# Modulation vectors summed on VectorE instead of TensorE, their weights in a ring of four tiles, and every high part of a weight made by ScalarE

## The chip, the cores and the metric

One NeuronCore of a Trainium2 chip runs the whole program. The metric is the device time of one execution in microseconds. Five engines work side by side, each with its own queue, in order: TensorE (PE; its weight loads are shown as PEld), VectorE (DVE), ScalarE (ACT), GpSimd (POOL) and SyncE (SP), which here issues the DMA transfers. TensorE reads SBUF and writes PSUM; a PSUM tile of this kernel holds 1024 fp32 columns, and there are four of them.

## The reference

A two-layer trunk is run on 640 tokens: 128 context tokens and 512 latent tokens. Each group has its own conditioning vector, and each layer makes six modulation vectors of 1024 numbers from it, for both groups:

```python
def adaln(cond, w, b):
    m = jax.nn.silu(cond) @ w + b                      # w: 1024 x 6144, per layer
    return [m[:, None, i * D_MODEL:(i + 1) * D_MODEL] for i in range(N_MOD)]

def trunk_layer(x, mods, l, P, angs, ctx_k, ctx_v):
    sh1, sc1, g1, sh2, sc2, g2 = mods
    hn = rmsnorm(x, P['norm1_g'][l]) * (1 + sc1) + sh1
    mix, k, v = token_mixer(hn, l, P, angs, ctx_k, ctx_v)   # attention, Fourier mixer, gates, w_o
    x = x + g1 * mix
    hn = rmsnorm(x, P['norm2_g'][l]) * (1 + sc2) + sh2
    return x + g2 * channel_mixer(hn, l, P), k, v           # w_up, 3-tap convolution, silu gate, w_down
```

All data are fp32. The modulation vectors depend on the two conditioning vectors alone, not on the tokens, so their product with w (24 MB per layer) can be made at any time before its use.

## The kernel before

Activations lie transposed, channels on partitions and the 640 tokens along the free axis, in two chunks of 320. A product of fp32 precision is made of three fp32r products: weight and activation are each split into a high part (the value rounded to fp32r) and a low part (the rest), and `proj` (line 358) issues for each block of 128 input channels and each chunk high x high, high x low and low x high into PSUM: six matmuls of 320 columns per block of input channels. After each such block it calls `tick` (line 348), the clock of all side work.

Weights come in blocks of mostly 1 MB in the order of `make_plan` (line 71) through two raw tiles (`pump_loads`, line 286). `queue_split` (line 298) lists, for each 512 columns of the next block, one function that makes the high part `w_h` (line 311 on ScalarE, line 313 on GpSimd) and one that makes the low part `w_l` by subtraction on VectorE (line 317). A tick issues one of them, and one function of the queue `q` of epilogues. During the attention ScalarE makes all high parts; elsewhere ScalarE and GpSimd take turns.

```python
self.hcount += 1
if self.heads_on or self.hcount % 2:
    nc.scalar.copy(out=h[:, a:b], in_=raw[:, a:b])
else:
    nc.gpsimd.tensor_scalar(out=h[:, a:b], in0=raw[:, a:b], scalar1=1.0, scalar2=0.0, ...)
```

The modulation vectors are cut in blocks of 512 columns, 12 per layer. The first four of layer 0 are made in the prologue. The other 20 are made here by `ada_half` (line 399): a half holds 512 of the 1024 input channels, which come as one 1 MB block through the same raw tiles as the weights. Four matmuls with the conditioning vectors as weights (128x32, of which two columns are used) lie side by side in four column strips of the array and stream 512 columns each, in fp32; the profile shows two instructions for each. The first half's sums are copied to SBUF (line 407), the second's added (line 411); then four transposes, a reduction over the strips (line 429) and the addition of the bias (line 416) give four columns of `c_mods` for both groups. 12 halves lie in each layer's attention, four in each layer's gates, and the eight of the four blocks that layer 1's first norm needs lie in layer 0's feed-forward part, one after each up-projection job from the second on.

A layer runs so (`layer`, line 1244): attention, eight heads of five units each, whose steps (scores, softmax on VectorE and ScalarE, transposes, product with the values) alternate with the projections for the next head as filler by a written cost; then the gates stage, eight jobs of two projections each, with the Fourier mixer's steps between them; `merge` (Fourier and attention projections and the gates' products); `w_o` with the update of x; the feed-forward part, eleven pairs of up-projection jobs (22 tiles of 128 channels for values, 22 for gates) with the convolution (line 945 on ScalarE, line 940 twice on VectorE), and down-projections in three rounds after the fifth, eighth and eleventh pair. At the three norm boundaries `hold` keeps new splits back while the norm's steps run.

In the gates the projections alternate between the two PSUM tiles `ps_d`, and a sigmoid (line 786) frees each; the Fourier mixer uses the other two. In the merge and feed-forward parts projections go round all four tiles (`psq`).

The other intermediate tiles are 53 numbered slots of 640 columns, handed out first in, first out by `alloc` and `give`. The tables (rotary cosine and sine, Fourier matrices) have a tile of their own, `c_big`, loaded once by one DMA. The code's order is a priority and not yet the queues': a list scheduler under the tile framework orders each engine's queue, so that an instruction whose inputs are there can stand ahead of one that the code issues earlier.

Of the kernel before, what the change touches and what calls it, by code (L numbers as in the profile page):

```python
# [12 lines left out]
AF = mybir.ActivationFunctionType  # L13
# [14 lines left out]
NSLOT = 53  # L28
# [3 lines left out]
FILL = (1.3, .5, 1.1, 1.1)  # L32
FF_ROUNDS = ((0, 8), (8, 6), (14, 8))
# [37 lines left out]
def make_plan():  # L71
# [10 lines left out]
    def ada(l, cb):  # L82
        return [(("ada", l, cb, r), "ada", "w_ada", l, 512 * r, 4, [(512 * cb, 512)]) for r in range(2)]

# [6 lines left out]
    def ada_next():  # L91
        if adaq:
            add(*adaq.popleft())

    adaq = deque()
    for l in range(DEPTH):
        kq(l, 0)
        v(l, 0)
        for cb in range(4, 12):
            adaq.extend(ada(l, cb))  # L100
        for h in range(8):
            if h < 7:
                kq(l, h + 1)
                ada_next()
                if h < 6 and h % 2 == 0:
                    v(l, h // 2 + 1)
                    ada_next()
            else:
                for i in range(2):
                    w(("f", l, i), "w_in", l, 0, 8, [(256 * i, 256)])  # L110
                    ada_next()
        for i in range(4):
            for g in range(2):
                w(("g", l, g, i), "w_in", l, 0, 8, [(3584 + 1024 * g + 256 * i, 256)])
                ada_next()
        assert not adaq
# [6 lines left out]
        if l == 0:  # L123
            for cb in (2, 3, 0, 1):
                adaq.extend(ada(1, cb))

        def up(j):
            for g in range(2):
                w(("up", l, g, j), "w_up", l, 0, 8, [(DFF * g + 256 * j, 256)])
                if j:  # L130
                    ada_next()
# [16 lines left out]


# [11 lines left out]
def lay_out(inputs):  # L161
# [4 lines left out]
    for l in range(DEPTH):  # L166
# [7 lines left out]
        "w_first": np.stack([np.stack([block(g, src, 4) for src in b]) for b in FIRST_ADA]),  # L174
        "w_stream": np.concatenate([block(g, src, shape[0]).reshape(-1) for _, src, shape, _ in make_plan()]),
# [8 lines left out]
class Kern:  # L184
    def __init__(self, tc, st, I, O):
# [9 lines left out]
        self.big = mk("c_big", [128, 2560])  # L195
        self.ident = self.small
        b = self.big
        self.cos, self.sin = b[:, 0:512], b[:, 512:1024]
        self.csj = b[:, 1024:1280]
        self.c128, self.s128 = b[:, 1280:1408], b[:, 1408:1536]  # L200
        self.ttab = [b[:, 1536 + 256 * i:1792 + 256 * i] for i in range(4)]
        self.one = mk("c_one", [128, 1])
# [16 lines left out]
        self.q = deque()  # L219
        self.plan = make_plan()  # L220
# [5 lines left out]
        self.wseq = [i for i in range(self.n) if self.plan[i][3] == "w"]  # L226
# [6 lines left out]
        self.hcount = 0  # L233
        self.heads_on = False
        self.out_job = None
        self.psi = 0

# [60 lines left out]
    def queue_split(self, j):  # L298
# [1108 lines left out]
```

## Time and profile before

| | |
|---|---|
| median of 3 runs | 2242.63 us (2241.78 to 2243.69) |
| profiled execution, its own time | 2242.44 us |
| its span, first to last instruction | 2240.7 us |
| mean granted TensorE clock | 0.994 of 2.4 GHz |
| busy: PE / PEld | 2185.7 us (98%) / 2102.7 us (94%) |
| busy: DVE / ACT / POOL | 1225.3 (55%) / 800.2 (36%) / 362.4 us (16%) |
| DMA | 200.41 MB, mean 89 GB/s |

The stages of the span, in us: prologue to 72, attention of layer 0 to 380, gates to 500, merge and w_o to 672, feed-forward to 1126, boundary to 1170, attention of layer 1 to 1480, gates to 1600, merge and w_o to 1772, feed-forward to the end. Busy times of engines overlap; that of PE counts from a matmul's start to its modelled end, and matmuls are pipelined, so neighbours overlap too. An engine's idle time costs nothing as long as another engine sets the end.

### The profile page before, as it was taken

The page shows a single profiled execution, that of the slowest core. Times are in us where ns is not written, and L with a number is a line of the kernel's source. Part 1 is how long each engine was busy: PE and PEld are TensorE (multiplying, and loading weights), DVE is VectorE, ACT ScalarE, POOL GpSimd, SP SyncE. Part 2 cuts the span into 40 slices and gives each one's busy share as a digit, 9 for nine tenths or more (in the row PEclk, how much of TensorE's full clock was granted, in tenths as well). Part 3 has the DMA queues.
Part 4 walks back from the last instruction along what each step waited for, and adds up shares of the span by engine and source line. Part 5 has one row for each costly group of instructions (what it writes and reads, how often), then busy time and mean ns, then how long its engine had stood idle before and what let it go on. Part 6 is the DMA issues. An engine that isn't in the chain of part 4 may idle for free.

```text
span 2240.7 us, 36749 instructions
## 1 busy us (share of the span) xinstructions
PE 2185.7 (98%) x15142; PEld 2102.7 (94%) x15142; DVE 1225.3 (55%) x2258; ACT 800.2 (36%) x1601; POOL 362.4 (16%) x560
## 2 busy tenths in 40 slices
PE   7999999999999999999999999999999999999998
PEld 5988989999999999999989888899999999999997
DVE  5776675225456544545476766742344765355454
ACT  4565564212134221313246666532211433122221
POOL 2122122001032000000051211210010410000001
PEclk9999999999999999999999999999999999999999
DMA  8222322222213332122212222222222122222221
GB/s 312 84 84 84 118 79 76 113 94 71 73 66 113 133 112 76 62 90 76 76 66 102 83 82 85 79 112 99 91 76 76 59 76 75 75 77 75 76 76 47
DMA packets 40631, 200.41 MB, mean 89 GB/s; under 512 B 4496, under 2 KB 12048, under 8 KB 19344
## 3 DMA queue, kind: packets, MB, share of 16 engines
q1 hardware_dynamic: 40464, 198.07, 25.1%
q8 instruction: 119, 1.95, 0.4%
q14 instruction: 48, 0.39, 0.1%
HBM read 193.33 MB, written 4.72 MB: 88 GB/s over the span
## 4 chain that ended last, share of the span: by engine, by line
PE 76%; issue 7%; DVE 5%; POOL 5%; ACT 5%; DMA 1%; SPq 0%; POOLq 0%; ACTq 0%; DVEq 0%
PE ps_d L267 43%; PE ps_t L267 16%; PE ps_s L267 16%; POOL slot L500 2%; POOL ors L703 1%; ACT slot L634 1%; PE ps_t L270 1%; DVE nm L632 1%; DMA slot<-in_w_first 1%; ACT slot L536 1%; ACT junk L701 1%; DVE slot L515 1%; POOL oms L702 1%; ACT slot L537 1%; DVE w_l L317 1%
## 5 line engine op out<-in xcount | busy, mean ns | idle before, releaser
L267 PE MATMUL ps_d<-slot,w_h 128*128 128x320 f32 x5056 | 983.5, 313 | 8.0 <-DVE slot L501 4.5
L267 PEld LDWEIGHTS ps_d<-slot,w_h 128*128 128x128 f32 x5056 | 795.5, 188 | 25.0 <-DVE slot L501 8.4
L267 PE MATMUL ps_d<-slot,w_l 128*128 128x320 f32 x2528 | 595.6, 310 | 2.6 <-DVE w_l L317 2.6
L317 DVE TENSOR_TENSOR w_l<-w_raw,w_h 128x512 fp32r<-128x512 f32 x520 | 360.9, 704 | 264.5 <-ACT w_h L311 155.1
L267 PEld LDWEIGHTS ps_d<-slot,w_l 128*128 128x128 f32 x2528 | 427.8, 188 | 2.9 <-DVE w_l L317 2.9
L311 ACT CAST w_h<-w_raw 128x512 fp32r<-128x512 f32 x308 | 188.3, 620 | 460.2 <-PE ps_d L267 236.0
L313 POOL TENSOR_SCALAR w_h<-w_raw 128x512 fp32r<-128x512 f32 x212 | 143.8, 680 | 1216.5 <-PE ps_d L267 626.9
L267 PE MATMUL ps_s<-slot,w_h 128*128 128x320 f32 x1376 | 265.2, 310 | 0.0
L267 PE MATMUL ps_t<-slot,w_h 128*128 128x320 f32 x1376 | 264.6, 309 | 0.0
L267 PEld LDWEIGHTS ps_t<-slot,w_h 128*128 128x128 f32 x1376 | 217.7, 188 | 1.7 <-ACT slot L945 0.8
L267 PEld LDWEIGHTS ps_s<-slot,w_h 128*128 128x128 f32 x1376 | 217.5, 188 | 1.7 <-ACT slot L945 1.7
L634 ACT ACTIVATE slot<-ps_s,nm 128x640 f32<-128x640 f32 (+1 forms) x160 | 113.7, 711 | 150.2 <-DVE nm L632 148.3
L267 PE MATMUL ps_s<-slot,w_l 128*128 128x320 f32 x688 | 164.9, 310 | 1.1 <-DVE w_l L317 1.1
L267 PE MATMUL ps_t<-slot,w_l 128*128 128x320 f32 x688 | 164.7, 309 | 0.0
L632 DVE TENSOR_REDUCE nm<-ps_s 128x1 f32<-128x640 f32 (+1 forms) x160 | 113.9, 712 | 56.7 <-PE ps_s L267 49.6
L267 PEld LDWEIGHTS ps_s<-slot,w_l 128*128 128x128 f32 x688 | 116.9, 188 | 1.6 <-DVE w_l L317 1.6
L940 DVE SCALAR_TENSOR_TENSOR slot<-ps_d,c_vecs,slot 128x511 f32<-128x511 f32 (+1 forms) x176 | 84.6, 541 | 60.7 <-ACT slot L945 60.7
L267 PEld LDWEIGHTS ps_t<-slot,w_l 128*128 128x128 f32 x688 | 117.0, 188 | 0.0
L267 PE MATMUL ps_s<-slot,slot 128*128 128x320 f32 x512 | 102.3, 322 | 10.2 <-ACT slot L634 10.1
L267 PEld LDWEIGHTS ps_s<-slot,slot 128*128 128x128 f32 x512 | 77.7, 189 | 30.6 <-ACT slot L634 19.3
L267 PE MATMUL ps_d<-w_h,slot 128*128 128x256 f32 x480 | 99.6, 288 | 0.6 <-DVE cols L429 0.6
L940 DVE SCALAR_TENSOR_TENSOR slot<-ps_s,c_vecs,slot 128x511 f32<-128x511 f32 x88 | 42.6, 542 | 87.3 <-ACT slot L945 87.3
(167 smaller groups left out, 2258.9 us busy)
## 6 DMA issues: line engine op xcount, KB each, us to landing
w_raw<-in_w_stream SPq DMA_DIRECT2D x164, 1024.0 KB, 4.9
slot<-in_w_first SPq DMA_DIRECT2D x32, 256.0 KB, 6.0
w_raw<-in_w_stream SPq DMA_DIRECT2D x8, 768.0 KB, 4.3
slot<-in_x_t SPq DMA_DIRECT2D x8, 320.0 KB, 6.2
out_y_t<-slot SPq DMA_DIRECT2D x8, 320.0 KB, 2.2
c_big<-in_t_big SPq DMA_DIRECT2D x1, 1280.0 KB, 9.4
slot<-in_k_t SPq DMA_DIRECT2D x16, 64.0 KB, 1.8
slot<-in_v_h SPq DMA_DIRECT2D x16, 64.0 KB, 1.9
```

Source lines behind the costliest of these rows:

```text
L267: return self.nc.tensor.matmul(**a)
L270: return self.nc.tensor.transpose(*a)
L311: nc.scalar.copy(out=h[:, a:b], in_=raw[:, a:b])
L313: nc.gpsimd.tensor_scalar(out=h[:, a:b], in0=raw[:, a:b], scalar1=1.0, scalar2=0.0, op0=ALU.mult, op1=ALU.add)
L317: nc.vector.tensor_sub(out=lo[:, a:b], in0=raw[:, a:b], in1=h[:, a:b].bitcast(F32))
L500: (eng or nc.gpsimd).tensor_scalar(out=tmp[:, a:b], in0=tmp[:, a:b], scalar1=A, scalar2=B, op0=ALU.mult, op1=ALU.add)
L515: lambda: nc.vector.stream_shuffle(tmp[:, 128:640], src, mask=SHUF),
L536: nc.scalar.copy(out=KD[m][a:b], in_=kr[a:b])
L537: nc.scalar.copy(out=KD[m][c:d], in_=kr[a:b])
L632: nc.vector.tensor_reduce(out=st["nm"][:, m:m + 1], in_=s_ap, axis=AX.X, op=ALU.max, negate=True)
L634: nc.scalar.activation(out=p[:, 0:n], in_=s_ap, func=AF.Exp, bias=st["nm"][:, m:m + 1], scale=1.0, accum_out=st["sum"][:, m:m + 1])
L940: nc.vector.scalar_tensor_tensor(out=y[:, o0:o1], in0=ps[:, 192 + i0:192 + i1], scalar=w, in1=y[:, o0:o1], op0=ALU.mult, op1=ALU.add)
```

## The change

`make_plan` no longer holds blocks of w_ada, so the raw tiles carry weights alone. The 20 blocks of modulation vectors are computed as multiply-adds: a step takes a tile of 128 input channels by 512 columns, multiplies each partition by the conditioning number of that channel (one step per group) and adds it to an accumulator; after eight tiles the sum over the 128 partitions is left, and TensorE makes it for two blocks and both groups at once with a column of ones. The first tile of a block is written by ScalarE, the other seven are added by VectorE. The tiles come as 256 KB loads through a ring of four slots. A rate per tick sets how many steps are issued: 0.85 in the gates, 0.25 in layer 0's feed-forward part. Six blocks are made in layer 0's gates, eight in its feed-forward part, six in layer 1's gates, none in the attention. The high parts of all weights are made by ScalarE. The tables move into five slots, which are given back once used and loaded again for layer 1; the slots become 61.

```diff
-NSLOT = 53
+NSLOT = 61
 WARM = 7
 HOOKS = (1, 1.75)
 SECOND = (.25, .75)
 FILL = (1.3, .5, 1.1, 1.1)
+ADA_UPTO = ((6, 14), (20, 20))
+ADA_RATE = (.85, .25)
...
+ADA = [(0, cb) for cb in range(4, 12)] + [(1, cb) for cb in (2, 3, 0, 1)] + [(1, cb) for cb in range(4, 12)]
...
+    def tables(self):
+
+        b = self.big = [self.alloc() for _ in range(5)]
+        for i, t in enumerate(b):
+            self.nc.sync.dma_start(out=t[:, 0:512], in_=self.I["t_big"][:, 512 * i:512 * i + 512])
+        self.cos, self.sin = b[0][:, 0:512], b[1][:, 0:512]
+        self.csj = b[2][:, 0:256]
+        self.c128, self.s128 = b[2][:, 256:384], b[2][:, 384:512]
+        self.ttab = [b[3 + i // 2][:, 256 * (i % 2):256 * (i % 2) + 256] for i in range(4)]
...
-                self.hcount += 1
-                if self.heads_on or self.hcount % 2:
-                    nc.scalar.copy(out=h[:, a:b], in_=raw[:, a:b])
-                else:
-                    nc.gpsimd.tensor_scalar(out=h[:, a:b], in0=raw[:, a:b], scalar1=1.0, scalar2=0.0,
-                                            op0=ALU.mult, op1=ALU.add)
+                nc.scalar.copy(out=h[:, a:b], in_=raw[:, a:b])
...
+        self.beat += 1
+        self.ada_tick()
...
+    def ada_open(self, upto, rate):
+
+        self.ada_upto, self.ada_rate = 8 * upto, rate
+        if self.ada_n < self.ada_upto:
+            self.ada_ring = [self.alloc() for _ in range(4)]
+            self.ada_at = self.ada_n
+            for _ in range(4):
+                self.ada_load()
+
+    def ada_load(self):
+        n = self.ada_at
+        if n < self.ada_upto:
+            self.nc.sync.dma_start(out=self.ada_ring[n % 4][:, 0:512], in_=self.I["w_ada"][n // 8, n % 8])
+            self.ada_at += 1
+
+    def ada_step(self):
+
+        n, c = self.ada_n, self.ada_c
+        if n >= self.ada_upto:
+            return False
+        nc, w = self.nc, self.ada_ring[n % 4][:, 0:512]
+        b, k = divmod(n, 8)
+        if k == 0 and c == 0:
+            self.ada_acc += [self.alloc(), self.alloc()]
+        acc, x = self.ada_acc[2 * (b % 2) + c][:, 0:512], self.cs[:, k, c:c + 1]
+        if k == 0:
+            nc.scalar.activation(out=acc, in_=w, func=AF.Copy, scale=x)
+        else:
+            nc.vector.scalar_tensor_tensor(out=acc, in0=w, scalar=x, in1=acc, op0=ALU.mult, op1=ALU.add)
+        self.ada_c = 1 - c
+        if c:
+            self.ada_n += 1
+            self.ada_load()
+            if k == 7 and b % 2:
+                self.ada_sums.append((self.beat + 10, lambda b=b, acc=self.ada_acc: self.ada_rows(b - 1, acc)))
+                self.ada_acc = []
+            if self.ada_n == self.ada_upto:
+                self.give(*self.ada_ring)
+        return True
+
+    def ada_rows(self, b, acc):
+        nc = self.nc
+        ps, s = self.psq(), self.alloc()
         for j in range(4):
+            self.mm(out=ps[32 * j:32 * j + 32, 0:512], lhsT=self.one, rhs=acc[j][:, 0:512], tile_position=(0, 32 * j))
+        self.give(*acc)
+        nc.scalar.copy(out=s[:, 0:512], in_=ps[:, 0:512])
+        self.ada_sums.append((self.beat + 3, lambda: self.ada_columns(b, ps, s)))
+
+    def ada_columns(self, b, ps, s):
+        for j in range(4):
+            self.tr(ps[:, 512 + 128 * j:640 + 128 * j], s[:, 128 * j:128 * j + 128], self.ident)
+        self.give(s)
+        part = ps[:, 512:1024].rearrange("p (b g r) -> p b g r", b=4, g=4)
+        for i in range(2):
+            l, cb = ADA[b + i]
             bcol = self.vec[4][:, 48 * l + 4 * cb:48 * l + 4 * cb + 4]
+            self.nc.vector.tensor_tensor(out=self.mods[l][:, 4 * cb:4 * cb + 4, :], in0=part[:, :, 2 * i:2 * i + 2, 0],
+                                         in1=bcol.rearrange("p (j o) -> p j o", o=1).to_broadcast([128, 4, 2]), op=ALU.add)
+
+    def ada_until(self, n):
+
+        while self.ada_n < 8 * n and self.ada_step():
+            pass
+        while self.ada_sums:
+            self.ada_sums.popleft()[1]()
+
+    def ada_tick(self):
+        if self.ada_sums and self.beat >= self.ada_sums[0][0]:
+            self.ada_sums.popleft()[1]()
+        self.ada_credit += 0 if self.hold else self.ada_rate
+        if self.ada_credit >= 1:
+            self.ada_credit -= 1
+            self.ada_step()
...
-        cost = lambda h: 1.2 + (13.1 + (7.9 if h % 2 == 0 else 5.3) if h < 6 else 13.1 if h == 6 else 26.2)
+        cost = lambda h: (13.1 + (7.9 if h % 2 == 0 else 5.3) if h < 6 else 13.1 if h == 6 else 26.2)
...
+        self.give(*self.big[0:2])
...
+        self.ada_open(ADA_UPTO[l][0], ADA_RATE[0])
...
+        self.give(*self.big[2:5])
         some(1e9)
         self.flush()
         for pr in hn:
             self.give(*pr)
+        self.ada_until(ADA_UPTO[l][0])
         self.finish_a(l, 1)
         Z = self.merge(l)
         hn2 = [(self.alloc(F32R), self.alloc(F32R)) for _ in range(8)]
         hooks = self.w_o(l, Z, hn2)
+        self.ada_open(ADA_UPTO[l][1], ADA_RATE[1])
         self.ff = [None] * NFF
         self.up_first(l, hn2, hooks)
         for j in range(1, 5):
             self.up(l, j, hn2)
+        self.ada_until(8)
         self.down(l, 0)
...
         if l + 1 < DEPTH:
+            self.ada_until(ADA_UPTO[l][1])
+            self.tables()
             hn = [(self.alloc(F32R), self.alloc(F32R)) for _ in range(8)]
             self.finish_a(l + 1, 0)
```

Left out of the diff: the functions it removes (`ada_next`, `ada_half`, whose working is told above, and `psa`), their calls at the end of the projection jobs, and the new fields' first values. `ada_until` issues at once what is still to be made up to a block, and the sums that are due.

## Rows read from the trace of the kernel before

**Rows 1.** The page's first part, busy time by engine; its fourth, the chain.
```profile
PE 2185.7 (98%) x15142; PEld 2102.7 (94%) x15142; DVE 1225.3 (55%) x2258; ACT 800.2 (36%) x1601; POOL 362.4 (16%) x560
...
PE 76%; issue 7%; DVE 5%; POOL 5%; ACT 5%; DMA 1%; SPq 0%; POOLq 0%; ACTq 0%; DVEq 0%
```

**Rows 2.** Windows: length, busy PE, PEld, DVE, ACT, POOL, granted clock, DMA share, GB/s.
```profile
0.00:72.00 72.00, 58.32 (x343) 42.27 (x344) 43.75 (x99) 31.36 (x60) 19.16 (x32) 0.91 0.69 255
72.00:380.00 308.00, 296.66 (x2171) 276.29 (x2171) 211.92 (x416) 181.62 (x453) 63.39 (x109) 0.99 0.26 89
380.00:500.00 120.00, 120.00 (x817) 114.61 (x817) 28.48 (x61) 27.52 (x47) 10.22 (x21) 1.00 0.27 98
...
672.00:1048.00 376.00, 375.49 (x2561) 366.55 (x2560) 197.18 (x354) 99.08 (x138) 41.38 (x59) 1.00 0.27 96
1048.00:1126.00 78.00, 77.94 (x533) 77.68 (x532) 40.17 (x72) 19.71 (x30) 5.97 (x9) 1.00 0.20 68
1126.00:1170.00 44.00, 40.04 (x280) 37.46 (x279) 33.21 (x61) 20.01 (x42) 30.19 (x38) 1.00 0.18 60
```

**Rows 3.** Line 945, layer 0, then layer 1: duration min/median/max, first to last start.
```profile
L945 ACT ACTIVATE slot<-ps_d,c_vecs x22: 868/886/890, 680.3 to 1065.1; 128x640 f32<-128x640 f32 x22
...
L945 ACT ACTIVATE slot<-ps_t,c_vecs x11: 875/889/890, 689.3 to 1079.2; 128x640 f32<-128x640 f32 x11
...
L945 ACT ACTIVATE slot<-ps_d,c_vecs x22: 882/886/890, 1782.0 to 2155.5; 128x640 f32<-128x640 f32 x22
...
L945 ACT ACTIVATE slot<-ps_t,c_vecs x11: 877/886/892, 1789.8 to 2169.6; 128x640 f32<-128x640 f32 x11
```

**Rows 4.** Timeline of layer 0's gates: start, length, engine, line, operation.
```profile
383.67 0.88 DVE L733 TENSOR_TENSOR slot<-slot 128x127 f32<-128x127 f32 x4
...
433.20 1.49 PE L267 MATMUL ps_s<-c_big,slot 128*128 128x128 f32 x10
...
454.92 1.06 PE L267 MATMUL ps_t<-w_raw,c_cond 128*32 128x512 f32 x8
...
455.92 0.86 PE L267 MATMUL ps_d<-slot,w_h 128*128 128x320 f32 x4
...
457.79 0.60 PE L270 MATMUL ps_t<-c_small,slot 128*128 128x128 f32 x4
...
458.14 0.83 PE L267 MATMUL ps_d<-slot,w_h 128*128 128x320 f32 x4
```

**Rows 5.** Window of instructions on the conditioning vectors: busy PE, PEld, ACT, POOL.
```profile
672.00:1048.00 376.00, 8.52 (x64) 1.26 (x64) 0.00 (x0) 0.00 (x0) 1.00 0.27 96
```

**Rows 6.** Groups by line and shape: busy us, mean ns, idle before and its releaser.
```profile
L646 DVE SCALAR_TENSOR_TENSOR slot<-slot,c,slot 128x640 f32<-128x640 f32 x64 | 57.9, 905 | 1.9
...
L646 DVE SCALAR_TENSOR_TENSOR slot<-slot,c,slot 128x128 f32<-128x128 f32 x16 | 5.6, 351 | 0.5
...
L786 ACT ACTIVATE slot<-ps_d 128x640 f32<-128x640 f32 x32 | 22.7, 708 | 85.3 <-PE ps_d L267 85.3
...
L311 ACT CAST w_h<-w_raw 128x512 fp32r<-128x512 f32 x308 | 188.3, 620 | 460.2 <-PE ps_d L267 236.0 <-PE ps_t L267 210.5 <-DMA w_raw<-in_w_stream 9.5
...
L313 POOL TENSOR_SCALAR w_h<-w_raw 128x512 fp32r<-128x512 f32 x212 | 143.8, 680 | 1216.5 <-PE ps_d L267 626.9 <-PE ps_t L267 430.6 <-DMA w_raw<-in_w_stream 102.4
```

**Rows 7.** The chain in order of time, one tile: start, length, work.
```profile
725.73 7.04 PE ps_t L267 x48
```

**Rows 8.** Waits of PE's weight loads, 72 to 380: total us, times, longest.
```profile
PEld ps_s L267 <- ACT slot L634: 9.3, 14, 2.1
PEld ps_t L270 <- DVE on L704: 7.5, 7, 1.7
```

**Rows 9.** DMA issues by line: count, KB each, median us to landing.
```profile
w_raw<-in_w_stream SPq DMA_DIRECT2D x164, 1024.0 KB, 4.9
slot<-in_w_first SPq DMA_DIRECT2D x32, 256.0 KB, 6.0
```

**Rows 10.** Waits of SyncE's queue: total us, times, longest.
```profile
SPq L291 <- DVE w_l L317: 1214.2, 110, 30.7
```

More of the change, by code (lines that the diff above doesn't have):

```diff
@@ L194, in __init__ @@
         self.small = mk("c_small", [128, 128])
-        self.big = mk("c_big", [128, 2560])
         self.ident = self.small
[L197 to L202, printed above, removed]
+        self.one = mk("c_one", [128, 32])
         self.mh = mk("c_mh", [128, 6])
@@ L225, in __init__ @@
         self.cur = 0
-        self.wseq = [i for i in range(self.n) if self.plan[i][3] == "w"]
+        self.wseq = list(range(self.n))
         self.wpos = {i: j for j, i in enumerate(self.wseq)}
@@ L329, in begin @@
         assert self.loaded > i
-        if kind == "ada":
-            return i, self.raw[i % 2].rearrange("p (k n) -> p k n", n=512)
         j = self.wpos[i]
@@ L388, in vtile @@
                 yield 0.66
-    def ada_next(self):
-        if self.plan[self.cur][3] != "ada":
-            return
-        _, l, cb, r = self.plan[self.cur][0]
-        i, raw = self.begin("ada", l, cb, r)
-        yield from self.ada_half(l, cb, r, [raw[:, j, :] for j in range(4)], lambda: self.finish_raw(i))
-    def ada_half(self, l, cb, r, w, after):
+    def ada_open(self, upto, rate):
[5 more added lines that the diff above has]
+                self.ada_load()
@@ L400, in ada_half @@
+    def ada_rows(self, b, acc):
         nc = self.nc
-        ps = self.psa()
+        ps, s = self.psq(), self.alloc()
         for j in range(4):
-            self.mm(out=ps[32 * j:32 * j + 32, 0:512], lhsT=self.cs[:, 4 * r + j, :], rhs=w[j], tile_position=(0, 32 * j))
-        after()
-        if r == 0:
-            self.half = self.alloc()
-            nc.scalar.copy(out=self.half[:, 0:512], in_=ps[:, 0:512])
-            yield 0.92
-            return
-        s = self.half
-        nc.vector.tensor_add(out=s[:, 0:512], in0=s[:, 0:512], in1=ps[:, 0:512])
@@ L413, in columns @@
-        def columns():
-            m = self.columns(ps, 512, s)
-            bcol = self.vec[4][:, 48 * l + 4 * cb:48 * l + 4 * cb + 4]
-            nc.vector.tensor_tensor(out=self.mods[l][:, 4 * cb:4 * cb + 4, :], in0=m,
-                                    in1=bcol.rearrange("p (j o) -> p j o", o=1).to_broadcast([128, 4, 2]), op=ALU.add)
-        self.q.insert(min(len(self.q), 1), columns)
-        yield 1.3
+            self.mm(out=ps[32 * j:32 * j + 32, 0:512], lhsT=self.one, rhs=acc[j][:, 0:512], tile_position=(0, 32 * j))
@@ L465, in rstd_cols @@
         for i, t in enumerate(starts):
-            self.mm(out=ps[:, c0 + i:c0 + i + 1], lhsT=self.acc[:, t:t + 128], rhs=self.one)
+            self.mm(out=ps[:, c0 + i:c0 + i + 1], lhsT=self.acc[:, t:t + 128], rhs=self.one[:, 0:1])
         ms, rs = self.tiny("ms", 6), self.tiny("rs", 6)
@@ L585, in kq_job @@
         self.later(*self.q_epi(ps, l, h))
-        yield from self.ada_next()
     def v_alloc(self, l, p):
@@ L620, in v_job @@
         self.v_epi(l, p, ps, 0, 4, 1)
-        yield from self.ada_next()
     def unit(self, l, h, qt):
@@ L966, in up @@
                 self.up_epi(l, g, m, ps, yv)
-            self.run(self.ada_next())
     def up_epi(self, l, g, m, ps, yv):
@@ L1147, in prologue @@
         w[3] = ada_load(3)
-        nc.sync.dma_start(out=self.big, in_=I["t_big"])
+        self.tables()
         kr = self.k_start(0, 0)
@@ L1354, in layer @@
         if l + 1 < DEPTH:
+            self.ada_until(ADA_UPTO[l][1])
+            self.tables()
             hn = [(self.alloc(F32R), self.alloc(F32R)) for _ in range(8)]
```

34 lines of the change are left out of this document (8 added, 26 removed).

## The prediction

> **What bounds the kernel now.** I read the page's first part first: TensorE is busy for 98% of the span, VectorE 55%, ScalarE 36%, GpSimd 16% [rows 1]. The chain of waits agrees: 76% of what ended last is TensorE [rows 1]. Then the busy time by stage: in the gates TensorE has no gap at all (120.00 of 120 us) while VectorE works 28.48 us, and late in the feed-forward part VectorE works 40.17 of 78; only the attention leaves TensorE idle, 11.3 us in layer 0 (308.00 less 296.66; I take layer 1's for the same), besides the start and the layer boundary [rows 2]. So work taken off TensorE shortens the span nearly one for one, as long as what takes its place stays beside TensorE's work. The sum below is made against the profiled execution, 2242.44 us (span 2240.7 and 1.7 around it); the median of the three runs is 2242.63, 0.2 above it.
>
> **Removed from TensorE.** 20 blocks of modulation vectors are computed in halves of four matmuls (eight instructions), and after the second half come four transposes. The price is read best where the two layers differ by this alone: the feed-forward part of layer 0 holds four blocks, that of layer 1 none. From the first convolution activation to the last it takes 1079.2 - 680.3 = 398.9 us in layer 0 and 2169.6 - 1782.0 = 387.6 in layer 1 (first start in ps_d, last start in ps_t) [rows 3]. The 11.3 us between them are 2.83 per block. The timeline gives the bare issue as a lower bound: a half takes 454.92 to 455.92, 1.00 us, four transposes 457.79 to 458.14, 0.35, so 2.35 per block [rows 4]; the rest is the switch in and out. I take 2.83 throughout: 20 x 2.83 = 56.5 us off (bound 47.0).
>
> **Added to TensorE.** Ten sums over partitions, one for two blocks, each of the shape of one half and four transposes: at least 1.00 + 0.35 = 1.35, at most 2.83 - 1.00 = 1.83. I take the middle, 1.6: 16.0 us (13.5 to 18.3).
>
> Here a rule of the Trainium skill speaks against this sum. The trace: in the main stretch of layer 0's feed-forward part the matmuls on the conditioning vectors have 8.52 us of matmul busy time, but 1.26 us of weight loads [rows 5]. The Trainium skill, page "Trainium Kernel Development and Optimization", section "Performance Expectations", calls matmul busy time a bad measure because matmuls are pipelined, and goes by the share of weight loads. What that would give stands as the third rival. The layer-to-layer difference of 11.3 us, which is no busy time of either kind, is on the side of the 8.52.
>
> **Moved to VectorE and ScalarE.** Per block 16 steps: two on ScalarE, 14 multiply-adds on VectorE, 128x512 from two SBUF operands. The trace has this instruction at 640 columns (905 ns) and 128 columns (351 ns) [rows 6]; between them 512 columns come to 351 + 384/512 x 554 = 767 ns. In the gates of each layer six blocks are made, 84 multiply-adds, 64.4 us, beside the 28.48 of before: 93 of 120 us. The stage has 8 jobs x 16 = 128 ticks, and at 0.85 per tick the 96th step is issued at tick 113, the last sum at 123, its transposes at 126: they end inside the stage. A tile of eight ticks takes 7.04 us [rows 7], so a tick is 0.88, in which VectorE gets 0.85 x 14/16 x 0.767 = 0.57 us of new work. In the feed-forward part of layer 0 there are eight blocks, 112 multiply-adds, 86 us over some 454 us, of which VectorE works 197.18 + 40.17 = 237 now [rows 2]: 323 of 454. Neither stage fills the engine, so I cost the steps themselves at nothing. The cover is the slack of the weight splits: the trace shows that the queues run far ahead of the code's order (the last small Fourier additions of layer 0 run at 383.67, the group of matmuls that uses them at 433.20 [rows 4]), so a multiply-add in front of a split delays it without TensorE seeing it. If that cover fails, the slow rival below has the price.
>
> The sums need a PSUM tile. In the gates two of the three take one of the two tiles in which the gate projections alternate. Where the sum falls inside a tile, the next projection has to wait for the sigmoid of the one just ended, 0.708 us [rows 6] and the signals; one such turn in a layer, with margin 1.0 us each: 2.0 us (0 to 4).
>
> **The burst before the last down-projection.** From the release of the first feed-forward job on, layer 0 has 16 + 128 + 64 + 96 + 48 + 96 = 448 ticks, at 0.25 that is 112 steps; 128 are wanted. The last block's 16 steps are therefore issued in one go, 14 x 0.767 = 10.7 us on VectorE, and then a sum, its copy (0.6, as a conversion of 128x512 has [rows 6]) and its transposes. With nothing to hide it TensorE stands for 10.7 + 1.35 + 0.6 = 12.7 us; with queues that run ahead, and VectorE idle for 37.8 of the 78 us before [rows 2], for nothing. The rows are nearer to the second: I take 3.0 (0 to 12.7).
>
> **Attention.** 12 halves leave each layer's attention, 6 x 2.83 = 17.0 us. Here TensorE isn't alone: its weight loads wait 9.3 us per layer for the exponentials and 7.5 for the normalised outputs [rows 8]. The removed work was filler between these steps, so a part comes back as longer waits, and all of it (17.0) would if the softmax chain were the bound. It isn't as yet: 11.3 us idle in 308. I take a fifth, 3.4 per layer, 6.8 us (0 to 34).
>
> **Weight splits all on ScalarE.** 212 conversions move from GpSimd (680 ns) to ScalarE (620 ns) [rows 6]: 131 us more on ScalarE, which is 36% busy. Outside the stage boundaries they hide behind the splits' lead. At the start ScalarE, 31.36 of 72 us, gets GpSimd's turns of the first three blocks, two each (3.7 us); at the layer boundary GpSimd, 30.19 of 44 us busy [rows 2], loses two turns per job of 14 us, six in 44 (4.1 us), while the norm waits on it. I take 0 for both (-4 to +4). The tables' move into five pool tiles costs five loads in place of one at the start, and five more before the last down-projection of layer 0; the tables are wanted in layer 1's first epilogue, a whole stage later: nothing.
>
> **Loads.** The same 160 tiles' bytes come as 256 KB pieces through a ring of four. A ring lasts 8 steps / 0.85 x 0.88 = 8.3 us in the gates; a 256 KB load lands in 6.0 us in the crowd of the start [rows 9]. That fits, so nothing; it is the place where the slow rival sits.
>
> **Sum:** 2242.4 - 56.5 + 16.0 + 2.0 + 3.0 + 6.8 = 2213.7, forecast 2214. Its own range: 2200 (no waits come back, and GpSimd's relief counts) to 2228 (half of the attention's 34, and 8 for the burst).
>
> **Rivals.**
> 1. The attention gives it all back. TensorE's removed filler turns into waits for exponentials: 2213.7 + 34 - 6.8 = 2241, no change. For it: the waits for exponentials and outputs exist today [rows 8] and VectorE is at 212 of 308 us there. Against: they sum to under 17 us a layer, and VectorE and ScalarE also lose work. Chance 0.07.
> 2. Slower: the ring starves. The ring's loads stand in SyncE's queue with the 1 MB weight loads, and these wait there for VectorE's splits, 1214.2 us in all [rows 10]. If each turn of the ring lands behind one 1 MB load, it takes 4.9 + 6.0 = 10.9 us [rows 9] against 8.3: 2.6 late, and VectorE stands in front of multiply-adds while splits queue behind. 96 tiles in the gates are 24 turns, 62 us: 2276. It decides from 33/24 = 1.4 us per turn on, where 2247 is passed. For it: VectorE takes its queue in order. Against: 48 tiles, 12.6 MB, in 113 ticks add 127 GB/s to the gates' 98, less 35 for the four halves that leave: 190, and the start moves 255 [rows 2]. Chance 0.09.
> 3. The gain is as small as the weight loads say. 64 instructions have 1.26 us of them [rows 5], so 320 have 6.3; the sums add 80, 1.6; 40 transposes fewer, at 0.35 for four [rows 4], give 3.5. Gain 8.2, time 2234. This is what the rule of the Trainium skill cited above comes to. Against it is the 11.3 us of four blocks alone. Chance 0.05.
>
> **How the numbers follow.** The forecast has 0.79, rival 1 0.07, rival 2 0.09, rival 3 0.05. About 0.2% (4.5 us) is what a measurement of this kernel can tell from no change. Faster: 0.79 and 0.05, less 0.01 for a forecast whose waits all come at once: 0.83. Same: rival 1 and a mild ring, 0.09. Slower: 0.08. The range is the forecast's own, 1 us wider below and 4 above, where the burst's upper bound and the third rival lie: 2199 to 2232.
>
> **What would show it.** Right: the feed-forward part of layer 0, measured as in [rows 3], takes 387.6 + 4 x 1.6 + 3 = 397 at most, and TensorE's gates stage shrinks by five us less one wait; the attention by 12 to 17; VectorE near 93 of 120 in the gates. Wrong: TensorE waits on w_l or on Fourier inputs in the gates, multiply-adds waiting for ring loads by microseconds (rival 2), exponentials' waits doubled (rival 1), or a gap of over 8 us before the last down-projection of layer 0.

## The result, and the profile after

The changed kernel takes 2203.19 us (median of 4 runs, 2200.95 to 2204.87) against 2243.16 for the kernel before beside it: ratio 0.9821, 95% interval 0.9804 to 0.9838. The profiled run takes 2202.99 us, span 2201.2; the forecast was 2214. First the page of the changed kernel: busy times, then the chain of waits [rows 1].

```profile
PE 2152.5 (98%) x14862; PEld 2095.2 (95%) x14862; DVE 1374.7 (62%) x2498; ACT 935.7 (43%) x1843; POOL 230.6 (10%) x348
...
PE 78%; DVE 6%; ACT 6%; POOL 5%; issue 4%; DMA 0%; SPq 0%; ACTq 0%; DVEq 0%; POOLq 0%
```

TensorE lost 33 us of busy time, VectorE got 149, and TensorE is busy for as large a share as before: the span shrank with its work. Where, is read best between events that every kernel here has: the first and last exponential of a layer's attention, the last product of its merge (line 844), the first and last convolution activation (line 971). The windows of the changed kernel between these, with the columns of [rows 2]; the cuts at 661.4, 1054.2 and 1742.3 answer [rows 3]:

```profile
0.00:71.00 71.00, 61.52 (x362) 44.24 (x363) 44.93 (x104) 37.57 (x73) 15.06 (x26) 0.95 0.73 266
71.00:351.10 280.10, 272.98 (x2001) 262.78 (x2001) 195.82 (x374) 172.30 (x439) 56.11 (x91) 1.00 0.17 56
351.10:575.10 224.00, 222.29 (x1509) 216.47 (x1508) 136.04 (x233) 75.32 (x127) 13.10 (x23) 1.00 0.36 117
575.10:661.40 86.30, 82.57 (x551) 82.05 (x551) 51.51 (x97) 33.48 (x63) 21.81 (x26) 0.96 0.27 92
661.40:1054.20 392.80, 392.80 (x2683) 389.29 (x2685) 271.98 (x470) 144.81 (x215) 0.00 (x0) 1.00 0.36 115
1054.20:1156.70 102.50, 96.37 (x663) 94.10 (x656) 58.70 (x111) 43.48 (x84) 26.36 (x32) 0.97 0.20 68
...
1661.40:1742.30 80.90, 80.50 (x551) 79.71 (x550) 44.86 (x87) 30.97 (x60) 21.12 (x26) 1.00 0.20 66
1742.30:2130.20 387.90, 387.90 (x2647) 387.90 (x2646) 206.46 (x360) 135.52 (x200) 0.00 (x0) 1.00 0.23 77
```

The same stages of the main kernels, in us, each the difference of two such start times (L0, L1: layers 0 and 1):

| stage | before | E1 splits alone | E2 vectors alone | changed | E4 held | E5 turned | E6 both |
|---|---|---|---|---|---|---|---|
| start | 74.6 | 70.4 | 76.2 | 71.0 | 71.1 | 73.3 | 71.6 |
| attention L0 | 298.5 | 299.1 | 280.9 | 280.1 | 280.6 | 280.1 | 280.5 |
| gates to merge L0 | 224.4 | 224.7 | 224.1 | 224.0 | 224.0 | 224.0 | 224.0 |
| w_o, norm L0 | 82.8 | 81.2 | 87.8 | 86.3 | 82.8 | 86.6 | 82.7 |
| feed-forward L0 | 398.9 | 399.1 | 392.5 | 392.8 | 390.8 | 392.7 | 390.8 |
| boundary | 98.8 | 95.9 | 103.9 | 102.5 | 101.2 | 96.4 | 96.4 |
| attention L1 | 296.8 | 296.8 | 280.7 | 280.6 | 280.9 | 280.7 | 280.8 |
| gates to merge L1 | 224.4 | 224.7 | 224.1 | 224.1 | 224.0 | 224.0 | 224.0 |
| w_o, norm L1 | 82.8 | 81.0 | 82.7 | 80.9 | 80.9 | 80.9 | 80.8 |
| feed-forward L1 | 387.6 | 387.9 | 387.6 | 387.9 | 387.8 | 387.8 | 387.9 |
| end | 71.1 | 70.5 | 70.5 | 71.0 | 70.8 | 71.1 | 70.1 |

The attentions give 18.4 and 16.2 us. The feed-forward part of layer 0 gives 6.1, and two stages lost: 3.5 around layer 0's second norm, 3.7 at the boundary. Each of the two holds one long wait, here in the timeline of the changed kernel (a number in brackets is the engine's idle time just before, with what ended it):

```profile
640.84 0.72 PE L261 MATMUL ps_s<-c_one,slot 128*128 128x1 f32 x6
...
642.21 3.40 DVE L408 SCALAR_TENSOR_TENSOR slot<-slot,c_cond,slot 128x512 f32<-128x512 f32 x5
...
645.52 0.16 DVE L498 TENSOR_SCALAR ms<-ps_s 128x3 f32<-128x3 f32 x1
645.59 2.07 DVE L408 SCALAR_TENSOR_TENSOR slot<-slot,c_cond,slot 128x512 f32<-128x512 f32 x3
645.77 1.29 POOL L499 TENSOR_TENSOR rs<-ms,c_mh 128x3 f32<-128x3 f32 x1 [7.80 <-DVE ms L498]
...
647.11 1.65 PE L261 MATMUL ps_s<-c_small,rs 128*128 128x128 f32 x6 [3.67 <-POOL rs L499]
...
1112.39 0.54 DVE L868 SCALAR_TENSOR_TENSOR slot<-ps_d,c_mods,slot 128x320 f32<-128x320 f32 x1
...
1112.62 0.46 PE L261 MATMUL ps_s<-slot,w_h 128*128 128x320 f32 x2
...
1114.91 0.49 DVE L531 TENSOR_TENSOR slot<-slot,slot 128x320 fp32r<-128x320 f32 x1 [0.33 <-POOL slot L530]
...
1116.15 0.76 DVE L531 TENSOR_TENSOR slot<-slot,slot 128x320 fp32r<-128x320 f32 x1 [0.75 <-POOL slot L530]
1116.83 0.54 DVE L868 SCALAR_TENSOR_TENSOR slot<-ps_d,c_mods,slot 128x320 f32<-128x320 f32 x1
...
1117.42 0.90 PE L261 MATMUL ps_d<-slot,w_h 128*128 128x320 f32 x2 [3.67 <-DVE slot L868]
...
1118.39 0.73 PE L261 MATMUL ps_d<-slot,w_h 128*128 128x320 f32 x2
```

The norm's sums end on TensorE at 641.56 (640.84 and 0.72), and VectorE's next step (line 498, 0.16 us) needs nothing else. But at 642.21 five multiply-adds of the feed-forward part stand ahead of it in VectorE's queue, although the code issues them later: the queues are ordered ahead of time, and these were ready. The step starts at 645.52. In the second wait the addition that clears a tile d, at 1116.83, stands behind normalised outputs (line 531) that wait for GpSimd.

Behind each wait TensorE is slow for a while: two matmuls of 320 columns take 0.46 us at 1112.62 and 0.73 at 1118.39. Windows of the changed kernel before and after the second wait:

```profile
1104.00:1114.00 10.00, 9.75 (x68) 9.41 (x66) 7.83 (x17) 8.97 (x21) 6.75 (x10) 1.00 0.08 23
1117.40:1123.00 5.60, 5.58 (x21) 5.58 (x22) 5.25 (x10) 3.01 (x6) 1.02 (x2) 0.50 0.27 110
```

The granted clock is 1.00 (2.4 GHz) ahead of the wait and 0.50 (1.2 GHz) for the 5.6 us behind it. An estimate from these rows: 3.67 us of waiting and half of 5.6 us, 6.5 us in all.

### The profile page after: what moved, and what is told of

Its sections match the earlier page's. It is cut to its first block, busy times and chain, and to the rows that moved or that the text cites. A ratio compares the mean times of both kernels' runs of the same rounds, so it can differ in the third digit from the quotient of the medians.

```text
span 2201.2 us, 36709 instructions
## 1 busy us (share of the span) xinstructions
PE 2152.5 (98%) x14862; PEld 2095.2 (95%) x14862; DVE 1374.7 (62%) x2498; ACT 935.7 (43%) x1843; POOL 230.6 (10%) x348
## 4 chain that ended last, share of the span: by engine, by line
PE 78%; DVE 6%; ACT 6%; POOL 5%; issue 4%; DMA 0%; SPq 0%; ACTq 0%; DVEq 0%; POOLq 0%
PE ps_d L261 44%; PE ps_s L261 17%; PE ps_t L261 16%; POOL ors L731 2%; PE ps_t L264 2%; ACT slot L662 2%; POOL slot L530 2%; DVE nm L660 1%; ACT junk L729 1%; DVE on L732 1%; ACT slot L529 1%; POOL oms L730 1%; ACT slot L566 1%; DVE slot L545 0%; ACT slot L715 0%
## 5 line engine op out<-in xcount | busy, mean ns | idle before, releaser
L261 PE MATMUL ps_d<-slot,w_h 128*128 128x320 f32 x5088 | 995.4, 313 | 5.9 <-DVE slot L868 3.7
L261 PE MATMUL ps_d<-slot,w_l 128*128 128x320 f32 x2544 | 603.6, 310 | 1.8 <-DVE w_l L306 1.6
L303 ACT CAST w_h<-w_raw 128x512 fp32r<-128x512 f32 x520 | 318.6, 620 | 465.0 <-PE ps_d L261 248.1
L306 DVE TENSOR_TENSOR w_l<-w_raw,w_h 128x512 fp32r<-128x512 f32 x520 | 355.0, 691 | 180.1 <-ACT w_h L303 177.9
L261 PE MATMUL ps_t<-slot,w_h 128*128 128x320 f32 x1344 | 259.7, 310 | 0.5 <-DVE slot L531 0.3
L408 DVE SCALAR_TENSOR_TENSOR slot<-slot,c_cond,slot 128x512 f32<-128x512 f32 x280 | 197.8, 749 | 8.9 <-DMA slot<-in_w_ada 8.0
L261 PE MATMUL ps_s<-slot,slot 128*128 128x320 f32 (+2 forms) x592 | 114.5, 318 | 2.8 <-ACT slot L662 1.4
L499 POOL TENSOR_TENSOR rs<-ms,c_mh 128x3 f32<-128x3 f32 (+1 forms) x9 | 8.6, 954 | 960.2 <-DVE ms L498 960.2
L261 PEld LDWEIGHTS ps_s<-slot,slot 128*128 128x128 f32 x592 | 87.3, 188 | 12.7 <-ACT slot L662 10.7
```

Source lines behind the costliest of these rows:

```text
L261: return self.nc.tensor.matmul(**a)
L306: nc.vector.tensor_sub(out=lo[:, a:b], in0=raw[:, a:b], in1=h[:, a:b].bitcast(F32))
L408: nc.vector.scalar_tensor_tensor(out=acc, in0=w, scalar=x, in1=acc, op0=ALU.mult, op1=ALU.add)
```

## The experiments

**E1 and E2: the two halves of the change alone.** E1 is the kernel before with one edit; E2 is the changed kernel with the old turns put back.

```diff
-                if self.heads_on or self.hcount % 2:
-                    nc.scalar.copy(out=h[:, a:b], in_=raw[:, a:b])
-                else:
-                    nc.gpsimd.tensor_scalar(...)
+                nc.scalar.copy(out=h[:, a:b], in_=raw[:, a:b])
```

> The kernel before with one edit: all high parts of weights on ScalarE. Theory: this edit alone gives the shorter start (74.6 -> 71.0 us to the first exponential of layer 0) and nothing in the attentions, the gates and the first feed-forward part: 2239 us, 3.6 under before. If the new wait of TensorE for a down-projection's tile (3.7 us at the layer boundary, VectorE's additions standing behind normalised outputs that GpSimd makes) comes of this edit too, the boundary grows by 3.7 (98.8 -> 102.5) and the sum is 2242.6, no change. Rival: the shorter start and the boundary come of the new modulation vectors (the tables in five loads, the other order of loads); then this kernel stays within 1 us of before in every stage. The attention stays at 298.5 and 296.8 us in the first case and in the second.

> The changed kernel with the old turns of ScalarE and GpSimd for high parts: the modulation vectors alone. Theory: the attentions stay at 280 us, as of the changed kernel (the 17 us a layer come of the halves that left), the start goes back to 74.6, the layer boundary to 98.8: 2203.2 + 3.6 - 3.7 = 2203, the same as the changed kernel. Rival: GpSimd's relief in the gates and the feed-forward part is a condition of the gain (VectorE's two-operand steps and GpSimd's conversions disturb each other): then the multiply-adds take longer than 749 ns, GpSimd's conversions longer than 680, and the gates and the first feed-forward part grow by more than 3 us each, 2210 or more.

E1: 2232.46 us against 2241.62, ratio 0.9958 (0.9945 to 0.9970). E2: 2213.52, ratio 0.9873 (0.9860 to 0.9887). They add: 9.2 and 28.1 make 37.3, where the whole change gives 38 to 40. So the splits' move alone is worth a quarter of the gain. By the table its gain lies at the start (4.2), at both second norms (1.6, 1.8) and at the boundary (2.9), nowhere else; my theory had the start alone. The boundary's new wait is no child of the splits: E2 has it too, and the one of the norm as well. TensorE's longest wait in E2 around layer 0's second norm, then at the boundary (total us, times, longest):

```profile
PE ps_s L263 <- POOL rs L506: 3.9, 1, 3.9
```
```profile
PE ps_d L263 <- DVE slot L875: 3.9, 2, 2.8
```

The norm of layer 1, which no modulation step touches, first in the window of the kernel before, then of E1:

```profile
1699.20:1782.00 82.80, 81.15 (x551) 79.75 (x550) 46.49 (x87) 25.70 (x49) 27.68 (x36) 1.00 0.19 64
```
```profile
1691.90:1772.90 81.00, 80.63 (x551) 79.73 (x551) 44.89 (x87) 30.97 (x59) 21.11 (x26) 1.00 0.20 66
```

GpSimd is free of ten conversions (36 instructions to 26), and TensorE's gaps fall from 1.65 us to 0.37. TensorE's waits in these two windows, before and in E1:

```profile
PE ps_d L267 <- DVE slot L842: 0.6, 1, 0.6
PE ps_s L267 <- DVE w_l L317: 0.6, 1, 0.6
PE ps_d L267 <- DVE slot L501: 0.5, 2, 0.3
```
```profile
PE ps_d L267 <- DVE slot L496: 0.3, 1, 0.3
```

A wait for a low part of a weight goes, one for an addition that clears a tile goes, and those for normalised outputs shrink. Whether the norm's steps had stood behind conversions in GpSimd's queue, or the conversions had come late behind the norm's steps, no run separates.

In E2 conversions and multiply-adds run side by side. Group rows of E2: the multiply-adds, and the conversions on GpSimd, which had taken 680 ns [rows 6]:

```profile
L415 DVE SCALAR_TENSOR_TENSOR slot<-slot,c_cond,slot 128x512 f32<-128x512 f32 x280 | 203.3, 768 | 10.3 <-DMA slot<-in_w_ada 8.8 <-ACT slot L413 0.8
...
L309 POOL TENSOR_SCALAR w_h<-w_raw 128x512 fp32r<-128x512 f32 x212 | 155.1, 732 | 1173.1 <-PE ps_d L263 582.5 <-PE ps_s L263 402.6 <-PE ps_t L263 64.8
```

Both grew as the rival said (768 for 749 ns, 732 for 680), but the gates and the feed-forward part did not (224.1, 392.5): the 10 us between E2 and the changed kernel lie at the start (5.2) and the norms (1.5, 1.4, 1.8), as E1 has them.

**E9: where the splits' gain sits.** The kernel before, with the flag for ScalarE alone set at the start, from `w_o` to the end of `up_first`, and from the last down-projection of layer 0 on.

> The kernel before with the high parts on ScalarE alone at the start and around the norms (from the w_o product to the end of the first feed-forward job, and from the last down-projection of layer 0 on); in the gates and the rest of the feed-forward part ScalarE and GpSimd take turns as before. Theory: the 9.2 us that the splits' move gives lie in GpSimd's relief while it makes the norms' lower halves, so this small part of the move gives all of it: 2233, with 70 to 71.5 us at the start, 81 after the gates, 96 at the boundary. Rival: what helps is ScalarE's shorter conversion (620 against 680 ns) along the whole kernel; then it gives no more than a third: 2239.

2233.66 us against 2241.90, ratio 0.9961 (0.9947 to 0.9974); start 71.9, norms 81.0, boundary 96.0. 42 of the 212 conversions (170 stay on GpSimd) give as much as E1 within the intervals: 2.7 us at the start and 6.4 at the two second norms and the boundary. So the gain doesn't come of a shorter conversion along the whole kernel.

**E3 and E4: the burst, and the second norm.** E3 has 0.29 in place of 0.25 in `ADA_RATE`. E4 has 0.30; the first modulation steps of the feed-forward part read their factor through a copy that needs the last normalised output, and their ring is opened behind the first up-projections and no longer ahead of them:

```diff
-        self.ada_open(ADA_UPTO[l][1], ADA_RATE[1])
         self.ff = [None] * NFF
         self.up_first(l, hn2, hooks)
+        if l == 0:
+            self.nc.vector.scalar_tensor_tensor(out=self.csg, in0=hn2[7][1][:, 638:640].bitcast(F32), scalar=0.0,
+                                                in1=self.cs[:, 0, 0:2], op0=ALU.mult, op1=ALU.add)
+            self.gate_at = self.ada_n // 8
+        self.ada_open(ADA_UPTO[l][1], ADA_RATE[1])
```

> The changed kernel with 0.29 steps per tick in the feed-forward part in place of 0.25: 130 steps in 448 ticks, so no block is issued in a burst before the last down-projection. Theory: the burst was already hidden (the last sum runs at 1053.84, four jobs of TensorE ahead of the layer boundary), so nothing changes: 2203 within 2 us, and the 3.7 us wait for the down-projection's tile stays. Rival, the prediction's term: the burst costs 3 us or more and the boundary's wait comes of it: 2199.5, and the boundary from 102.5 to 99 us.

> As the run with 0.29, at 0.30, and the feed-forward part's modulation steps can't start before the last normalised output of the second norm is there (their first factor is read through a copy that needs it; the values are the same). Theory: the 3.7 us wait of TensorE for the second norm (behind the power on GpSimd, which took 1.29 us with multiply-adds around it, and behind eight multiply-adds in VectorE's queue) goes, and the clock in this stretch is back to 1.00: the stretch from the gates' end to the first convolution activation goes from 86.3 to 83 us, time 2199.5. Rival: TensorE's wait comes of something else in the norm (rows, ScalarE with the extra conversions); then it stays at 86 and the time at 2203. In layer 1, which has no modulation steps there, it is 80.9 in either case.

E3: 2203.27 us, ratio 0.9827 (0.9813 to 0.9840): nothing. In the changed kernel the last multiply-add of layer 0 starts at 1015.2, in E3 at 941.7, both ahead of the last convolution activation (1054): the burst was covered. E3 has the wait at the norm too (3.7 us, to 649.02), but behind it the granted clock is full, as this window of E3 shows, so a wait of this length isn't always followed by the slow stretch:

```profile
649.00:655.00 6.00, 5.97 (x42) 5.98 (x43) 4.16 (x9) 3.77 (x7) 3.26 (x4) 1.00 0.44 145
```

E4: 2198.27, ratio 0.9804 (0.9791 to 0.9817). The norm's wait is gone, as its timeline shows:

```profile
642.85 0.15 DVE L502 TENSOR_SCALAR ms<-ps_s 128x3 f32<-128x3 f32 x1
...
643.09 0.85 POOL L503 TENSOR_TENSOR rs<-ms,c_mh 128x3 f32<-128x3 f32 x1 [4.49 <-DVE ms L502]
...
643.99 0.93 PE L263 MATMUL ps_s<-c_small,rs 128*128 128x128 f32 x6
```

The step is no longer behind multiply-adds, GpSimd's power takes 0.85 us and not 1.29, and TensorE goes on with no gap; the same six matmuls behind the power take 0.93 us where they took 1.65. The stretch falls from 86.3 to 82.8 and the feed-forward part by 2.0 more: in E4 13 matmuls (551 to 564, 2683 to 2670 in the two windows) have moved across the cut between them, so the 5.5 us belong together. The edit holds the steps back in two ways, by the copy and by the later ring; it shows that they caused the wait, not which of the two was needed. The windows of E4, with a granted clock of 1.00 where the changed kernel has 0.96:

```profile
575.70:658.50 82.80, 82.39 (x564) 81.56 (x563) 46.25 (x90) 32.12 (x62) 21.13 (x26) 1.00 0.22 77
658.50:1049.30 390.80, 390.80 (x2670) 387.33 (x2672) 275.16 (x477) 145.57 (x217) 0.00 (x0) 1.00 0.37 120
```

The 0.44 us between the two powers go with the three multiply-adds that run beside the longer one. A rule of the Trainium skill fits: by the page "SBUF — State Buffer", section "SBUF: two separate sides", a VectorE instruction with two SBUF inputs and a GpSimd instruction that reads SBUF exclude each other. The trace agrees in kind (1.29 against 0.85 us here, 732 against 680 ns in E2); no run separates it from other causes.

**E5 and E6: the boundary.** `psq` deals the PSUM tiles in the order d, d, s, t. In the gates the four halves took four; three sums take three, so what follows meets other tiles. E5 adds one turn, which puts back the place in the rotation and nothing else:

```diff
         self.ada_until(ADA_UPTO[l][0])
+        self.psi += 1
         self.finish_a(l, 1)
```

> The changed kernel with one step added to the rotation of the PSUM tiles (d, d, s, t) at the end of the gates. The gates took four tiles for halves before and take three for sums now, so every later stage of a layer meets other tiles than before; at the layer boundary, where the next layer begins at a fixed place of the rotation, TensorE now waits 3.7 us for VectorE to clear a tile d. Theory: this shift is the cause of that wait: the boundary goes from 102.5 to the 96 us of the run with the splits alone (95.9), the rest stays: 2197. Rival: the wait comes of the modulation vectors' work near the boundary (five loads for the tables, the last block's steps, the addition's place in VectorE's queue); then the boundary stays at 101 to 103 and the time at 2203. The stretch after the gates keeps its 86 us in either case.

> The run that holds the modulation steps back behind the second norm (0.30 per tick) with the step in the rotation as well. Theory: both gains add, since they lie in different stretches: 2198.3 less 5 to 6 at the boundary: 2193. Rival as for the step alone: 2198.

E5: 2197.90 us against 2242.18, ratio 0.9803 (0.9789 to 0.9816); the boundary falls from 102.5 to 96.4, as expected. TensorE's longest waits there, in E5:

```profile
PE ps_d L261 <- DVE slot L531: 1.3, 3, 0.7
PE ps_s L261 <- ACT slot L636: 1.1, 1, 1.1
PE ps_s L261 <- DVE w_l L306: 0.2, 1, 0.2
```

The wait of 3.67 us isn't among them, and the window of E5 that lies where the changed kernel was slow has the full clock:

```profile
1116.00:1126.00 10.00, 9.80 (x72) 9.57 (x71) 8.07 (x16) 3.29 (x7) 5.51 (x9) 1.00 0.34 119
```

The boundary is 6.1 us shorter, near the 6.5 estimated above.

E6, both edits: 2191.76 us, ratio 0.9776 (0.9763 to 0.9789), 11 us under the changed kernel; the two gains add. It is the best version here.

**E7: the price of a sum.** Each sum's four matmuls twice (`for j in (0, 1, 2, 3, 0, 1, 2, 3)`).

> The changed kernel with the four matmuls of each of the ten sums issued twice (the second writes the same values over the first). Theory: four such matmuls cost TensorE their issue, 1.06 us as the sum of layer 0's last two blocks shows for its eight instructions: 2203 + 10 x 1.06 = 2213.8. Rival, by weight loads: eight instructions have 8 x 0.02 = 0.16 us of these: 2203 + 1.6 = 2204.8, not to be told from no change.

2210.93 us, ratio 0.9863 (0.9849 to 0.9876): 7.7 us over the changed kernel, 0.8 for one sum's matmuls and less than the theory's 1.06. Each stage from gates to merge grows by 2.6 us (226.6 and 226.7), 0.87 for each of its three sums. The timeline of E7 has the doubled sum, and that of the changed kernel the single one:

```profile
411.32 1.92 PE L261 MATMUL ps_d<-slot,c_one 128*32 128x512 f32 x16
```
```profile
411.91 1.06 PE L261 MATMUL ps_d<-slot,c_one 128*32 128x512 f32 x8
```

Eight instructions more take 0.86. By weight loads the ten sums would have cost 1.6 us; the measurement is near the matmuls' issue and decides against the third rival for this shape. The Trainium skill, page "Trainium Kernel Development and Optimization", section "Performance Expectations", speaks of how close a kernel is to its roofline, and names MFU (the share of peak arithmetic) beside weight loads; to take it as the price of a few instructions was my reading, and that reading fails here.

**E8: the ring.** Two tiles in place of four.

> The changed kernel with a ring of two tiles in place of four. In the gates a tile of the ring is used up every 2 / 0.85 x 0.88 = 2.07 us, a turn of two tiles lasts 4.15, and in it fit two multiply-adds (1.5) and a load that lands 2.9 us after its issue: 4.4. Theory: VectorE starves by some 0.3 us per tile, 48 tiles, 14 us in each gates stage, but the stage has 120 us, of which it works 93, and the steps that come late end in the 14 ticks left: 2203 to 2208, with multiply-adds that wait for loads up from 8 us to 30 or more. Rival (the prediction's slow case): the waits stand in VectorE's queue ahead of the splits, and TensorE sees them: 2220 or more, the gates from 224 to over 232 us.

2201.07 us, ratio 0.9816 (0.9802 to 0.9829). VectorE's waits for the ring, in the changed kernel and in E8:

```profile
DVE slot L408 <- DMA slot<-in_w_ada: 8.0, 8, 2.3
```
```profile
DVE slot L408 <- DMA slot<-in_w_ada: 52.6, 36, 4.4
```

45 us more of waiting at the head of VectorE's queue, and TensorE sees none of it: gates to merge 223.6 and 222.6 us.

**E10: does the attention hide work of TensorE?** The kernel before, the four matmuls of each half in the attentions twice.

> The kernel before with the four matmuls of each half in the attentions issued twice (the second writes the same values): 12 halves a layer, at the bare issue of 1.00 us that the timeline of before shows for one. Theory: the attention gives nothing back in either direction, TensorE's own work sets its length: each attention grows by 12 x 0.88 (the price that the doubled sums showed) to 12 x 1.00, 10.5 to 12 us, 298.5 -> 309.5: 2264 in all. Rival, the prediction's term: a fifth of it is taken up by waits for exponentials that get shorter: 8.4 to 9.6 us a layer, 2259.

2265.22 us, ratio 1.0105 (1.0091 to 1.0119). The two attentions grow by 9.0 and 11.4 us, the span by 22.8, the rest in the stages behind them; the time by 23.3 for 24 halves, 0.97 each. The rival's 2259 lies below every run: over the whole kernel TensorE's extra work lengthens the span nearly one for one (0.97 us a half for a bare issue of 1.00). By the attentions alone it is less clear: layer 0's 9.0 lies in the rival's range of 8.4 to 9.6, layer 1's 11.4 in the theory's.

**E11: how far VectorE covers.** Each multiply-add twice, the copy into a spare tile.

> The changed kernel with each multiply-add on VectorE issued twice (the copy writes a spare tile): 280 more, 749 ns each, 210 us of VectorE. It tells how far the cover reaches that let the prediction cost these steps at nothing. Theory: from the last exponential to the merge's end VectorE works 136 of 224 us now and would work 199; what the gates' 120 us can't hold (28 + 129 of 120) runs on into the Fourier output and the merge, which need only the splits; in the first feed-forward part it is 272 + 84 of 393. So TensorE stays covered but for the sums that now come late, ahead of the merge: up to 5 us per layer, 2203 to 2215. Rival: splits queue behind the multiply-adds as soon as VectorE is full within the gates: 37 us late per layer, 2240 to 2275, with TensorE waiting for w_l.

2231.30 us, ratio 0.9947 (0.9934 to 0.9961): 28 us over the changed kernel, between the two theories. Gates to merge take 239.3 and 238.7 us (15 more each), the feed-forward part of layer 0 takes 392.8 as before, with 84 us more on VectorE. TensorE's waits from 351 to 600, in E11:

```profile
PE ps_t L261 <- ACT slot L246: 5.0, 1, 5.0
PE ps_t L261 <- DVE slot L247: 3.5, 1, 3.5
```

The doubled multiply-adds start from 351.1 to 501.4, where the single ones had ended at 437.6, and the splits of the merge's inputs come late: line 247 queues among them on VectorE, and line 246 on ScalarE waits for one of them. Of the 15 us 8.5 are waits, and the granted clock is 0.77 from 480 to 510.

## Why the prediction was near, and where its steps were off

The direction and most of the mechanism held; the sum came out 10.7 us high: terms mis-sized to one side (the attention's return, the burst, the splits) outweighed two costs that it lacked. By its steps, against the profiled run:

- *Removed from TensorE, 2.83 a block.* Held. E2's attentions are 17.6 and 16.1 us shorter, for 17.0 predicted from [rows 3].
- *Attention gives back 6.8 (0 to 34).* Mis-sized: nothing came back, E2's attentions are shorter by 33.7 of the 34.0. TensorE's weight loads waited less for the exponentials, not more: 9.3 us in [rows 8], now, from 71 to 351.1:

```profile
PEld ps_t L264 <- DVE on L732: 6.4, 12, 0.9
PEld ps_s L261 <- ACT slot L662: 5.2, 18, 0.5
PEld ps_t L264 <- DVE slot L674: 3.6, 6, 0.8
```

  E10 shows the same from the other side, over the whole kernel. The change also lowers the written cost by which filler is dealt out to each head by 1.2 (`cost` in the diff); no run separates what that did.
- *Ten sums 16.0, and 2.0 for turns.* Held. The feed-forward window of layer 0 has 36 instructions of TensorE more than layer 1's (2683 and 2647), three sums of twelve, and takes 4.9 us more: 1.63 a sum, for 1.6; the matmuls are 0.8 of it (E7). A gates stage gave 0.3 to 0.4 us where two blocks' 5.66 left, so its three sums and turns cost 5.3, for 5.8. My list of signs said that the gates would shrink by five us: that contradicted my own terms, which leave nearly zero there, and nearly zero it was.
- *The burst 3.0 (0 to 12.7).* Zero (E3).
- *All splits on ScalarE 0 (-4 to +4).* The term that failed: -9.2 (E1), outside its own bounds. I set ScalarE's extra turns at the start (3.7) as a cost against GpSimd's relief at the boundary (4.1) and let the two cancel, and I gave the second norms nothing. In E1 the start came out as a gain too (4.2), the boundary gave 2.9 and the two norms 3.4 together. E9 shows that these places hold the whole of it.
- *Steps on VectorE 0.* Right in the gates, with less than a factor of two in hand (E11), and in the feed-forward part behind its first job, with more; wrong at layer 0's second norm (below). The price was 749 ns for 767, as the page of the changed kernel has it, with the ring's loads below (their median to landing last):

```profile
L408 DVE SCALAR_TENSOR_TENSOR slot<-slot,c_cond,slot 128x512 f32<-128x512 f32 x280 | 197.8, 749 | 8.9 <-DMA slot<-in_w_ada 8.0
...
slot<-in_w_ada SPq DMA_DIRECT2D x160, 256.0 KB, 2.9
```

- *Ring 0.* Right, with a wide margin (E8); a load landed in 2.9 us, not the 6.0 that I used.
- *Missing: the norm's place in VectorE's queue, and the rotation of the PSUM tiles.* I said that queues run ahead of the code's order and took it as cover alone. It also put eight multiply-adds around the norm's short steps: E4 gives 5.0 back against E3, of which 3.7 was the wait itself. I counted how often sums take a tile, not that three in place of four shift every later tile: E5 gives 5.3 back.

Together: -6.8 (attention), -1.0 (gates, 0.5 a layer below my terms), -3.0 and -9.2, against +5.0 and +5.3, are -9.7 of the 10.7; the rest isn't assigned. So the nearness of the total is in part luck, errors of both signs: E6, which is the changed kernel without the two missing costs, takes 2191.76 us, 22 under the sum and outside the range of 2199 to 2232. Of the rivals, the first (the attention gives back) falls with E2 and E10, the second (the ring) with E8, the third with E7. One slip in the range: it is said to reach 2232 to take in the third rival, whose own sum is 2234. The start is not settled to better than 3 us: the changed kernel and its variants with the same code up to there (E3 to E8, E11) show 70.4 to 73.3. The kernels with GpSimd's turns at the start (before, E10, E2) show 74.2 to 76.2, so that a gain is there, but not its size.

## What to carry to other kernels

Work moved onto an engine with slack was free here except where a short step on the critical chain shares that engine: ask of each moved instruction whether it can be ready, and so stand in the queue, just ahead of a norm or an evacuation. A change in how many times tiles are taken from a rotation shifts all later users; look at the next fixed point of the rotation. And where two edits come together, price each by the stages in which its engine is waited for: GpSimd was 16% busy [rows 1], and its conversions around the norms and at the start still cost 8 to 9 us (E9, E1).

## What the runs showed of the hardware

GpSimd's power of 3 columns takes 0.85 us where VectorE is idle (E4) and took 1.29 beside multiply-adds. GpSimd's conversions took 680 ns on average before and 732 in E2, where multiply-adds run in the same stages, and the multiply-adds 768 ns there for 749. A wait of TensorE of 3.67 us at the changed kernel's boundary is followed by 5.6 us at a granted clock of 0.50, and the boundary without it is 6.1 us shorter (E5). A wait as long at E3's norm is followed by none of that (1.00 over the next 6 us). So the price of such a wait lay between its own length and nearly twice that.
